# A Hymba layer on one core: residual loads, stores and sums of the out-projection on other queues and engines

## The chip, the core and the metric

The kernel runs on one core of a Trainium2 chip. The metric is device time in microseconds (us). The core has TensorE (PE), VectorE (DVE), ScalarE (ACT), GpSimd (POOL) and SyncE (SP), each with its own instruction queue that is worked off in order. SP does nothing here but issue DMAs; GpSimd issues some DMAs beside its arithmetic.

## The reference

One layer of a Hymba decoder trunk, batch 1, 1024 tokens of width 1024 behind 16 meta tokens, all in fp32.

```python
h = concat([meta, x], axis=1)
u = rmsnorm(h, attn_norm_w)
gq, gk, gv, gz, gb, ga, fq, fk, fv, ff = split(u @ w_in)
o_gdn = gated_deltanet_group(concat([gq, gk, gv]), gz, gb, ga, ...)   # 4 heads of 128, chunked delta rule
o_fox = forgetting_attention_group(fq, fk, fv, ff, fgate_b)           # 8 heads of 64, softmax with a forget bias
h = h + concat([o_gdn, o_fox], axis=-1) @ w_out
h = h + swiglu(rmsnorm(h, ffn_norm_w), w_gate, w_up, w_down)          # hidden width 2816
return rmsnorm(h, final_norm_w)[:, N_META:]
```

The change touches the lines around `h + concat(...) @ w_out`. The two halves of that product, over `o_gdn` and over `o_fox`, are computed at different times.

## The kernel before

An fp32 product is made of three matmuls: each operand is split into a high and a low part (`split`, L165 on ScalarE and L166 on VectorE), and high x high, high x low and low x high are summed in PSUM. The stages, by their place in the profiled span: the first norm and in-projection, the gated-DeltaNet group up to about 430 us, attention from 435 to 580, the out-projection from there to about 658, and the feed-forward part to the end.

Tokens go in eight tiles of 128 (`tt`). Output columns go in two halves of 512 (`nb`). The order of TensorE's instructions is written out by hand, from a list of chains and fillers with estimated times (`od`). The other engines' order is set by a scheduler that simulates a timeline; `tc.issue_after(ins)` is a hint to it that what follows is issued after `ins`.

*During attention.* `scores` computes a block of scores into a PSUM tile `sc` (two of them in turn), VectorE reduces it into `pr` with a minimum `sm` (L1060), and ScalarE takes the exponential. Between these, TensorE is filled with the GDN half of the out-projection, `wout_gdn(nb, tt)`: a residual tile `ht` (five buffers) is loaded from `x` on GpSimd's queue (L1220), twelve matmuls make `wog`, VectorE adds it to `ht` (L1223), and GpSimd stores the sum to the array `h_d` in HBM (L1224). The eight tiles of `nb=0` and one of `nb=1` run there, and another after attention. The loads of the next head (`att_head`: `kk`, `sa`, `ka`, `qa`, `avt`, `vm`) are issued on SP.

*After attention.* For the tiles in the order 0, 4, 1, 5, 2, 6, 3, 7:

- `prep_load` loads attention's output `of` from `o_d` on SP (L1260); GpSimd adds its two halves (L1261). The last four of these sums are put off and run by `run_late`.
- `prep_pe` transposes the softmax's scales (`rbt`), VectorE multiplies them in (L1276), and the result is split into `ohl`.
- `load_h` loads the residual row `hst` on SP from `h_d` (L1287), or one half from `x` (L1284) and one from `h_d` (L1285).
- `out_fox(tt, nb)` makes the fox half of the product in a PSUM tile `wof` or `wx` (L204 to L206), VectorE adds it to `hst` (L1308); after the second half, `norm2` takes the sum of squares on ScalarE (L1183), a multiply-add `st_f` on VectorE (L219), a power on GpSimd (L220), and the normalized row `xn` on VectorE (L1185). The finished `hst` is stored to `h_d` on SP (L1312).
- `u_blocks(tt)` transposes `xn` (`u2t`, L1382) and splits the blocks that the feed-forward part reads (L1387, L1388 and the lines behind them).

`hst` has two buffers: tiles 0, 1, 2, 3 use one in turn, tiles 4, 5, 6, 7 the other. So a tile's load waits until the row of the tile before it in that buffer is stored. `wof` has two PSUM buffers.

In the rows of the orders below, a number behind a name tells its buffers apart: `ht_0_0` is the residual tile of `tt=0, nb=0`, `sc_0_0_1_0` a score tile of head 0, `st2_f4` the statistics of tile 4 in `norm2` (`st_f` in the trace), and `xn2_4` its normalized row (`xn`).

Of the kernel before, what the change touches and what calls it, by code (L numbers as in the profile page):

```python
# [21 lines left out]
NT = S // P  # L22
# [5 lines left out]
EPS = 1e-6  # L28
# [12 lines left out]
ORDER = (0, 4, 1, 5, 2, 6, 3, 7)  # L41
# [56 lines left out]
def tile_hymba_layer(ctx, tc, x, meta, attn_norm_w, w_in, conv_w, a_log, dt_bias, gdn_norm_w,  # L98
                     fgate_b, w_out, ffn_norm_w, w_gate, w_up, w_down, final_norm_w, out):
    nc = tc.nc  # L100
    x, out, w_in, conv_w = x[0], out[0], w_in[0], conv_w[0]
# [22 lines left out]
    def ps_v(name):  # L124
        return bank("pv", 2, name)
# [75 lines left out]
    def mm3(dst, pairs, first=True, last=True):  # L201
        n = len(pairs)
        for i, (lh, ll, rh, rl) in enumerate(pairs):
            nc.tensor.matmul(dst, lh, rh, start=(first and i == 0), stop=False)  # L204
            nc.tensor.matmul(dst, lh, rl, start=False, stop=False)
            nc.tensor.matmul(dst, ll, rh, start=False, stop=(last and i == n - 1))  # L206
# [3 lines left out]
    def mm3g(dst, pairs, us):  # L210
        n = len(pairs)
        for i, (lh, ll, rh, rl) in enumerate(pairs):
            for a, b, first, last in ((lh, rh, i == 0, False), (lh, rl, False, False), (ll, rh, False, i == n - 1)):
                nc.tensor.matmul(dst, a, b, start=first, stop=last)  # L214
                od.pe(us)
                yield

    def inv_rms(dst, ssq, n, scale, tmp):
        nc.vector.tensor_scalar(tmp, ssq, scale, EPS, op0=ALU.mult, op1=ALU.add)  # L219
        return nc.gpsimd.tensor_tensor(dst, tmp, mhalf[:tmp.shape[0], :n], op=ALU.pow)  # L220

    def bcast(ap, shape):
# [53 lines left out]
    def proj_tm(t, w, c0, n, name, tag=ps_mm):  # L276
        col, rows = tok_cols(t)
        acc = tag(name)
        mm3(acc[:rows, :n], [(uh[:, k, col:col + rows], ul[:, k, col:col + rows],
                              w[0][k][:, c0:c0 + n], w[1][k][:, c0:c0 + n]) for k in range(KT)])  # L280
        return acc
# [30 lines left out]
    for t in range(NT):  # L312
# [3 lines left out]
        acc = proj_tm(t, w, 0, 264, f"z1_{t}")  # L316
# [8 lines left out]
    acc = proj_tm(-1, w, 256, 8, "zg")  # L325
# [202 lines left out]
    V = nc.vector  # L528
# [199 lines left out]
    last, vst, fps = [None], [None], [fp]  # L728
# [103 lines left out]
    ra_ld = {}  # L832
# [344 lines left out]
    h_d = dram.tile([NT, P, D], F32, name="h_d")  # L1177

    xn_i = [None]

    def norm2(src, wb, dst, pool, nm):
        sst = pool.tile([P, 4], F32, tag="st2", bufs=2, name=f"st2_{nm}")
        nc.scalar.activation(dst, src, AF.Square, accum_out=sst[:, 0:1])  # L1183
        pw = inv_rms(sst[:, 2:3], sst[:, 0:1], 1, 1.0 / D, sst[:, 1:2])
        xn_i[0] = V.scalar_tensor_tensor(dst, src, sst[:, 2:3], wb, op0=ALU.mult, op1=ALU.mult)  # L1185
        return pw
# [1 line left out]
    def wout_w(k0, nb):  # L1188
        return w_out[P * k0:P * k0 + 256, 512 * nb:512 * nb + 512].rearrange("(k p) n -> p k n", p=P)

    wo0c = ExitStack()
    wo = wo0c.enter_context(tc.tile_pool(name="wo0", bufs=1))
    wvs = {}

    def wout_block(k0, nb, tiles=None, col=None):
        ws = ([], [])
        for i in range(2):
            hl = load_w([(wout_w(k0 + 2 * i, nb), 1024)], f"wo{k0}_{nb}{i}", tiles and tiles(i), col)
            for o, t in zip(ws, hl):
                o.extend(t[:, 512 * k:512 * k + 512] for k in range(2))  # L1200
        return ws

    def gdn_pairs(tt, nb):
        a, b, (wh, wl) = og_of("h", tt), og_of("l", tt), wvs[nb]
        return [(a[:, k], b[:, k], wh[k], wl[k]) for k in range(4)]

    h_st = []

    def wout_gdn(nb, tt):
        if nb not in wvs:  # L1210
            parts_n[0] = 2 if nb else 1
            with tc.issue_after(ra_ld[2].ins) if not nb else nullcontext():
                wvs[nb] = wout_block(0, nb, col=gnw)
            parts_n[0] = 1
            od.on("act", 2.2)
            od.on("dve", 3.2)
        cols, nbc = slice(P * tt, P * tt + P), slice(512 * nb, 512 * nb + 512)
        ht = wo.tile([P, 512], F32, tag="ht", bufs=5, name=f"ht_{tt}_{nb}")
        with tc.issue_after((h_st[-2] if len(h_st) >= 2 else last[0]).ins):
            nc.gpsimd.dma_start(ht, x[cols, nbc])  # L1220
        acc = ps_mm(f"wog_{tt}_{nb}")
        yield from mm3g(acc, gdn_pairs(tt, nb), 0.2135)
        V.tensor_add(ht, acc, ht)  # L1223
        h_st.append(nc.gpsimd.dma_start(h_d[tt, :, nbc], ht))  # L1224
        yield od.on("dve", 0.6)
# [3 lines left out]
    def wout_gdn_all(part):  # L1229
        for nb, tt in part:  # L1230
            yield from wout_gdn(nb, tt)
# [8 lines left out]
    G = nc.gpsimd  # L1240
# [2 lines left out]
    H = 512  # L1243
    RING = ("ohl_0", "ohl_1", "nwb", "hst_1", "xn2_1", "br", "ub")
    RAWS = {"g": ("hst_0", "of_0"), "u": ("xn2_0", "of_1")}
    turn, ofs, ofl, pre_u = {}, {}, {}, {}

    def wo_tile(tag, shape, bufs, nm, dt=F32, slot=None):
        turn[tag] = turn.get(tag, -1) + 1
        return wo2.tile(shape, dt, tag=slot or f"{tag}_{turn[tag] % bufs}", name=f"{tag}_{nm}")  # L1250

    late = []

    def run_late():
        while late:
            late.pop(0)()

    def prep_load(tt):
        of = wo_tile("of", [P, 8, P], 2, tt)
        ofl[tt] = nc.sync.dma_start(of, o_d[tt])  # L1260
        late.append(lambda: G.tensor_tensor(of[:, 0:4], of[:, 0:4], of[:, 4:8], op=ALU.add))  # L1261
        if len(ofs) < 4:
            run_late()
        sp_ = spread[:, len(ofs) % 2]
        nc.scalar.copy(sp_.rearrange("p m (i c) -> p (m i) c", i=2),
                       rinv[:, :, tt:tt + 1].broadcast_to([P, FH, DH]))
        ofs[tt] = of, sp_
# [11 lines left out]
        return tail[0]  # L1279

    def load_h(tt):
        ht = wo_tile("hst", [P, D], 2, tt)
        if tt in fused:
            nc.sync.dma_start(ht[:, H:], x[P * tt:P * tt + P, H:])  # L1284
            nc.sync.dma_start(ht[:, :H], h_d[tt, :, :H])  # L1285
        else:
            nc.sync.dma_start(ht, h_d[tt])  # L1287
        pre_u[tt] += (ht,)

    accs, last_h, pows2 = {}, [None], [None]  # L1290

    def fox_g(tt):
        if tt in fused:
            accs[tt] = bank("mm", 1, f"wx_{tt}")
            mm3(accs[tt], gdn_pairs(tt, 1), last=False)

    def pf_tile(i, nm, dt=F32R):
        return pfp.tile([P, D], dt, tag=f"pf{i}", name=nm)
# [1 line left out]
    xns = {}  # L1300

    def out_fox(tt, nb):
        oh, ol, ht = pre_u[tt]
        wv = wfs[nb]
        acc = accs[tt] if nb and tt in accs else ps_v(f"wof_{tt}_{nb}")
        mm3(acc, [(oh[:, k], ol[:, k], wv[0][k], wv[1][k]) for k in range(4)], first=not (nb and tt in accs))
        hb = ht[:, H * nb:H * nb + H]
        last_h[0] = V.tensor_add(hb, acc, hb)  # L1308
        if nb:
            xn = wo_tile("xn2", [P, D], 2, tt)  # L1310
            pows2[0] = norm2(ht, nwb2, xn, wo2, f"f{tt}")
            nc.sync.dma_start(h_d[tt], ht)  # L1312
            xns[tt] = xn

    for tag in RING + ("hst_0", "of_0", "xn2_0", "of_1", "s4"):
# [2 lines left out]

    nwb2 = wo2.tile([P, D], F32, tag="nwb", name="nwb2")
    spread = wo2.tile([P, 2, 4, P], F32, tag="s4", name="spread")  # L1320
    prep_load(ORDER[0])
    with tc.issue_after(last_o[0].ins):
        prep_load(ORDER[1])
# [6 lines left out]
    for _ in wout_gdn(1, 1):  # L1330
        pass
    first_o = prep_pe(ORDER[0])
    with tc.issue_after(first_o[0].ins), tc.issue_after(first_o[1].ins):
        wfs.append(wout_block(4, 1, lambda i: [pf_tile(2 * i + c, f"wf{c}_{i}") for c in range(2)]))
    with tc.issue_after(ofl[ORDER[1]].ins):
        load_h(ORDER[0])
    fox_g(ORDER[1])
    prep_load(ORDER[2])
    out_fox(ORDER[0], 0)
    prep_pe(ORDER[1])  # L1340
    with tc.issue_after(ofl[ORDER[1]].ins):
        load_h(ORDER[1])
# [224 lines left out]
    with tc.manual_schedule(engines={mybir.EngineType.PE}):  # L1567
        for i, tt in enumerate(ORDER):
# [150 lines left out]
        for n, p in enumerate(PH2):  # L1719
# [25 lines left out]
            late = [tc.issue_after(x.ins) for x in tail[0]] if p == "p4" else [nullcontext()] * 2  # L1745
# [31 lines left out]
```

## Time and profile before

| | |
|---|---|
| median of 3 runs | 1295.05 us (1294.88 to 1295.83) |
| profiled execution | 1295.79 us, its span 1294.1 us |
| mean granted TensorE clock | 0.997 of full speed |
| TensorE busy | 1276.2 us, 99% of the span |
| VectorE busy | 838.1 us, 65% |
| ScalarE busy | 548.1 us, 42% |
| GpSimd busy | 367.2 us, 28% |

A row of the timeline has the start in the span and the duration in us, the engine, the line of the kernel, the operation, what it writes and reads, and in brackets how long the engine had been idle and what released it. The table of stretches gives the busy time of each engine in a stretch, and the granted clock. Issuing a DMA counts as no busy time; "SPq" and "POOLq" are the queues in which DMAs are issued.

### The profile page before, as it was taken

To read this page: it belongs to the slowest core of one execution; us is meant where nothing else is said; L and a number is where in the kernel's file an instruction comes from. 1 tells how busy PE (TensorE), PEld (TensorE's weight loads), DVE (VectorE), ACT (ScalarE), POOL (GpSimd) and SP (SyncE) were. 2 spreads that over 40 slices of the span, in tenths; PEclk is the share of its full clock that TensorE was granted. 3 is DMA by queue.
4 is the path that set the end of the run, shared out by engine and by line. 5 is a ranking of instruction groups with operands and counts; after the bars stand their busy time and mean duration, and the time that the engine had idled before them with its cause. 6 is when DMAs were issued, how large, how long until landed. Compare 5 with 4: busy or idle time off the path is not lost.

```text
span 1294.1 us, 19940 instructions
## 1 busy us (share of the span) xinstructions
PE 1276.2 (99%) x7418; PEld 1125.9 (87%) x7418; DVE 838.1 (65%) x1511; ACT 548.1 (42%) x943; POOL 367.2 (28%) x343
## 2 busy tenths in 40 slices
PE   9999999999999999999999999999999999999998
PEld 8999999999999888887778888888888888888887
DVE  6567899465266588876887666655656654465645
ACT  6455434142234477874453323333333343433333
POOL 2012213102323222213405534455433443020301
PEclk9999999999999999999999999999999999999999
DMA  6433634666499678837434554554445467955513
GB/s 231 133 112 118 178 93 105 187 191 216 165 327 273 195 208 228 226 80 261 163 131 154 194 164 147 178 187 131 146 156 168 156 212 268 395 183 201 206 63 130
DMA packets 181840, 234.90 MB, mean 182 GB/s; under 512 B 19160, under 2 KB 132080, under 8 KB 178928
## 3 DMA queue, kind: packets, MB, share of 16 engines
q1 hardware_dynamic: 176048, 215.74, 52.1%
q0 software_dynamic: 5696, 17.90, 4.2%
q8 instruction: 58, 0.95, 0.3%
q14 instruction: 38, 0.31, 0.1%
HBM read 154.68 MB, written 78.92 MB: 181 GB/s over the span
## 4 chain that ended last, share of the span: by engine, by line
PE 87%; DVE 5%; DMA 3%; issue 2%; ACT 2%; SPq 1%; POOL 0%; POOLq 0%; DVEq 0%; ACTq 0%
PE xp L1658 9%; PE yp L1658 7%; PE ua L1483 5%; PE ga L1483 5%; PE gb L1483 5%; PE ud L1483 5%; PE gd L1483 5%; PE ub L1483 5%; PE pj_fq L214 4%; PE pj_fk L214 3%; PE pt L1101 2%; PE ue L1483 2%; PE ge L1483 2%; PE fv L214 2%; PE wog L214 2%
## 5 line engine op out<-in xcount | busy, mean ns | idle before, releaser
L166 DVE TENSOR_TENSOR al_p<-ra_p,ah_p 128x2048 fp32r<-128x2048 f32 (+1 forms) x21 | 47.2, 2250 | 95.1 <-ACT ah_p L165 95.1
L165 ACT CAST ah_p<-ra_p 128x2048 fp32r<-128x2048 f32 (+1 forms) x21 | 37.1, 1767 | 106.3 <-PE xp L1658 46.5
L1658 PE MATMUL xp<-wl_p,ah_p 128*128 128x512 f32 (+1 forms) x176 | 67.3, 382 | 0.0
L1658 PE MATMUL xp<-wh_p,al_p 128*128 128x512 f32 (+1 forms) x176 | 67.3, 382 | 0.0
L1658 PE MATMUL xp<-wh_p,ah_p 128*128 128x512 f32 (+1 forms) x176 | 67.3, 382 | 0.0
L1539 POOL TENSOR_TENSOR gzw<-gzw,uzt 128x512 f32<-128x512 f32 x11 | 18.1, 1649 | 169.7 <-DVE uzt L1528 113.0
L1483 PE MATMUL gb<-uh_p,w_g_p 128*128 128x512 f32 x176 | 57.8, 389 | 0.0
L1483 PE MATMUL ub<-uh_p,w_u_p 128*128 128x512 f32 x176 | 57.8, 389 | 0.0
L1483 PE MATMUL gd<-uh_p,w_g_p 128*128 128x512 f32 x176 | 57.8, 389 | 0.0
L1483 PE MATMUL ud<-uh_p,w_u_p 128*128 128x512 f32 x176 | 57.8, 389 | 0.0
L1539 POOL TENSOR_TENSOR gxy<-gxy,uxy 128x512 f32<-128x512 f32 x22 | 38.9, 1767 | 64.5 <-DVE uxy L1528 42.4
L165 ACT CAST ph<-pt 128x512 fp32r<-128x512 f32 (+1 forms) x96 | 45.4, 478 | 24.9 <-PE pt L1101 22.3
L166 DVE TENSOR_TENSOR pl<-pt,ph 128x512 fp32r<-128x512 f32 (+1 forms) x96 | 52.0, 553 | 4.5 <-ACT ph L165 4.0
L1065 ACT ACTIVATE pr<-pr,sm 128x144 f32<-128x144 f32 (+3 forms) x64 | 50.6, 793 | 9.6 <-DVE sm L1060 9.3
L166 DVE TENSOR_TENSOR w_u_p<-raw_u,w_u_p 128x512 fp32r<-128x512 f32 x42 | 41.0, 977 | 20.3 <-ACT w_u_p L165 20.1
L1483 PE MATMUL ga<-uh_p,w_g_p 128*128 128x512 f32 x160 | 52.5, 389 | 0.0
L1483 PE MATMUL ua<-uh_p,w_u_p 128*128 128x512 f32 x160 | 52.5, 389 | 0.0
L1658 PE MATMUL yp<-wh_p,ah_p 128*128 128x512 f32 x132 | 51.3, 389 | 0.0
L1658 PE MATMUL yp<-wl_p,ah_p 128*128 128x512 f32 x132 | 51.3, 389 | 0.0
L1658 PE MATMUL yp<-wh_p,al_p 128*128 128x512 f32 x132 | 51.3, 389 | 0.0
L165 ACT CAST w_u_p<-raw_u 128x512 fp32r<-128x512 f32 x42 | 26.0, 620 | 55.3 <-PE gd L1483 35.6
L166 DVE TENSOR_TENSOR wl_p<-rw_p,wh_p 128x2048 fp32r<-128x2048 f32 (+1 forms) x21 | 46.5, 2213 | 3.9 <-ACT wh_p L165 3.9
(654 smaller groups left out, 4246.2 us busy)
## 6 DMA issues: line engine op xcount, KB each, us to landing
ra_p<-ao_p SPq DMA_DIRECT2D x14, 1024.0 KB
raw_g<-in_w_gate_dram SPq DMA_DIRECT2D x22, 512.0 KB
raw_u<-in_w_up_dram SPq DMA_DIRECT2D x22, 512.0 KB
raw_d<-in_w_down_dram SPq DMA_DIRECT2D x22, 512.0 KB
wt_p<-raw_d SPq DMA_DIRECT2D x33, 256.0 KB
rw_p<-wt_p SPq DMA_DIRECT2D x8, 1024.0 KB
rw_p<-in_w_down_dram SPq DMA_DIRECT2D x6, 1024.0 KB
ao_p<-gzw SPq DMA_DIRECT2D x22, 256.0 KB
```

The lines of the kernel that those rows point to most:

```text
L165: cast = nc.scalar.copy(dst_hi, src)
L166: low = nc.vector.tensor_sub(dst_lo, src, dst_hi.bitcast(F32))
L214: nc.tensor.matmul(dst, a, b, start=first, stop=last)
L1065: nc.scalar.activation(pr[:, :n], pr[:, :n], AF.Exp, bias=sm[:, np_ - 1:np_], scale=-1.0, accum_out=rsum[:, h, j:j + 1])
L1101: nc.tensor.transpose(pt[:, P * j:P * j + P], pts[j][0][:, j, c0:c0 + P], ident)
L1483: nc.tensor.matmul(dst, a[:, c], b[:, k], start=(first and k == 0 and i == 0), stop=(k == 3 and i == 2), skip_group_check=not first)
L1539: last_mul[0] = G.tensor_tensor(gs[d], gs[d], us[d], op=ALU.mult)
L1658: nc.tensor.matmul(dst[:, n_], a[:, f, c], b[:, f, n_], start=(first and i == 0 and n == 0), stop=(i == NF - 1 and n == 2), skip_group_che ...
```

## The change

It has five parts, all around the residual and attention's output; TensorE's instructions and their order stay as they are.

1. The `ht` tiles of the first two blocks (`tt` 0 and 1, `nb` 0) are made before the second head's loads and loaded on SP ahead of them; before, they were loaded on GpSimd at the start of attention.
2. `load_h` of the first tile stands ahead of the `of` loads, without the hint that kept it behind the second of them.
3. The `h_d` stores of the first two tiles in the order (0 and 4) are issued on GpSimd instead of SP.
4. The sums of the halves of `of` for the last four tiles (2, 6, 3, 7) are made on VectorE, behind the `xn` that was made last, instead of on GpSimd.
5. The first add of the last tile (7) is issued behind the `st_f` multiply-add of tile 3.

```diff
+    ms_i = [None]
+
     def inv_rms(dst, ssq, n, scale, tmp):
-        nc.vector.tensor_scalar(tmp, ssq, scale, EPS, op0=ALU.mult, op1=ALU.add)
+        ms_i[0] = nc.vector.tensor_scalar(tmp, ssq, scale, EPS, op0=ALU.mult, op1=ALU.add)
         return nc.gpsimd.tensor_tensor(dst, tmp, mhalf[:tmp.shape[0], :n], op=ALU.pow)
...
+    wo0c = ExitStack()
+    wo = wo0c.enter_context(tc.tile_pool(name="wo0", bufs=1))
+
+    def ht_tile(tt, nb):
+        return wo.tile([P, 512], F32, tag="ht", bufs=5, name=f"ht_{tt}_{nb}")
+
+    ht01 = [ht_tile(tt, 0) for tt in range(2)]
+    with tc.issue_after(ra_ld[NT - 1].ins):
+        for tt in range(2):
+            nc.sync.dma_start(ht01[tt], x[P * tt:P * tt + P, 0:512])
     with tc.issue_after(last[0].ins):
         att_tiles(1)
     hds[1] = att_head(1)
...
-        ht = wo.tile([P, 512], F32, tag="ht", bufs=5, name=f"ht_{tt}_{nb}")
-        with tc.issue_after((h_st[-2] if len(h_st) >= 2 else last[0]).ins):
-            nc.gpsimd.dma_start(ht, x[cols, nbc])
+        if ht01:
+            ht = ht01.pop(0)
+        else:
+            ht = ht_tile(tt, nb)
+            with tc.issue_after(h_st[-2].ins):
+                nc.gpsimd.dma_start(ht, x[cols, nbc])
...
-        late.append(lambda: G.tensor_tensor(of[:, 0:4], of[:, 0:4], of[:, 4:8], op=ALU.add))
+
+        def halves_sum():
+            with tc.issue_after(xn_i[0].ins) if len(ofs) > 3 else nullcontext():
+                (V if len(ofs) > 3 else G).tensor_tensor(of[:, 0:4], of[:, 0:4], of[:, 4:8], op=ALU.add)
+
         if len(ofs) < 4:
-            run_late()
+            halves_sum()
+        else:
+            late.append(halves_sum)
...
-        last_h[0] = V.tensor_add(hb, acc, hb)
+        with tc.issue_after(ms_i[0].ins) if tt == ORDER[-1] and not nb else nullcontext():
+            last_h[0] = V.tensor_add(hb, acc, hb)
         if nb:
             xn = wo_tile("xn2", [P, D], 2, tt)
             pows2[0] = norm2(ht, nwb2, xn, wo2, f"f{tt}")
-            nc.sync.dma_start(h_d[tt], ht)
+            (nc.gpsimd if nst[0] < 2 else nc.sync).dma_start(h_d[tt], ht)
+            nst[0] += 1
...
+    load_h(ORDER[0])
     prep_load(ORDER[0])
...
-    with tc.issue_after(ofl[ORDER[1]].ins):
-        load_h(ORDER[0])
     fox_g(ORDER[1])
```

The scheduler's answer to it is seen in the order of instructions. VectorE at the start of attention, before:

```order
L1060 ISA sm_1_0_4_5067 128x1
L1223 TENSOR_TENSOR ht_0_0_5004<-wog_0_0_5006,ht_0_0_5004 128x512
L1060 ISA pr_1_0_5066,sm_1_0_4_5067<-sc_1_0_4_1_5075,zmask_5022,sm_1_0_4_5067 128x328
L1060 ISA sm_1_0_4_5067 128x1
L1060 ISA pr_1_0_5066,sm_1_0_5_5080<-sc_1_0_5_0_5081,zmask_5022 128x392
L1060 ISA sm_1_0_5_5080 128x1
L1223 TENSOR_TENSOR ht_1_0_5040<-wog_1_0_5042,ht_1_0_5040 128x512
```

And in the changed kernel, where `ht_0_0` is now:

```order
L800 SCALAR_TENSOR_TENSOR fhl_fq3_700_4981<-pj_fq3_700_4956,fhl_fq3_700_4981 128x340
L1236 TENSOR_TENSOR ht_0_0_4865<-wog_0_0_5008,ht_0_0_4865 128x512
L1072 ISA pr_0_0_5023,sm_0_0_0_5029<-sc_0_0_0_0_5030,zmask_5024 128x144
L1072 ISA sm_0_0_0_5029 128x1
L1072 ISA pr_0_0_5023,sm_0_0_1_5035<-sc_0_0_1_0_5036,zmask_5024 128x272
```

The first add has moved from behind the fifth score block to a place ahead of the first score reduction; the second add (`ht_1_0`) stays where it was.

GpSimd in the out-projection, at tiles 0 and 4, before:

```order
L1261 TENSOR_TENSOR of_4_7102<-of_4_7102 128x512
L1261 TENSOR_TENSOR of_1_7175<-of_1_7175 128x512
L220 TENSOR_TENSOR st2_f0_7220<-st2_f0_7220,mhalf_94 128x1
L1261 TENSOR_TENSOR of_5_7226<-of_5_7226 128x512
L220 TENSOR_TENSOR st2_f4_7323<-st2_f4_7323,mhalf_94 128x1
```

And in the changed kernel:

```order
L1277 TENSOR_TENSOR of_4_7104<-of_4_7104 128x512
L1277 TENSOR_TENSOR of_1_7175<-of_1_7175 128x512
L1331 DMA h_d_4995<-hst_0_7098 128x1024
L222 TENSOR_TENSOR st2_f0_7220<-st2_f0_7220,mhalf_94 128x1
L1277 TENSOR_TENSOR of_5_7226<-of_5_7226 128x512
L1331 DMA h_d_4995<-hst_4_7202 128x1024
L222 TENSOR_TENSOR st2_f4_7323<-st2_f4_7323,mhalf_94 128x1
```

Each of the two stores now stands between a sum of `of` and the power of `norm2`.

VectorE a little later, at tiles 1 and 5, before:

```order
L1185 SCALAR_TENSOR_TENSOR xn2_4_7322<-hst_4_7202,st2_f4_7323,nwb2_7096 128x1024
L1276 TENSOR_TENSOR of_5_7226<-rbt_5_7361,of_5_7226 128x512
L166 TENSOR_TENSOR ohl_5_7360<-of_5_7226,ohl_5_7360 128x512
L1308 TENSOR_TENSOR hst_1_7307<-wof_1_0_7346,hst_1_7307 128x512
L1308 TENSOR_TENSOR hst_1_7307<-wof_1_1_7375,hst_1_7307 128x512
```

And in the changed kernel:

```order
L1197 SCALAR_TENSOR_TENSOR xn2_4_7322<-hst_4_7202,st2_f4_7323,nwb2_7096 128x1024
L1327 TENSOR_TENSOR hst_1_7307<-wof_1_0_7346,hst_1_7307 128x512
L1295 TENSOR_TENSOR of_5_7226<-rbt_5_7361,of_5_7226 128x512
L166 TENSOR_TENSOR ohl_5_7360<-of_5_7226,ohl_5_7360 128x512
L1327 TENSOR_TENSOR hst_1_7307<-wof_1_1_7375,hst_1_7307 128x512
```

The first add of tile 1's residual row now stands ahead of the multiply of tile 5. On SP's queue its load (`hst_1`) stands ahead of the `of` load of tile 2 and of the residual loads of tile 5, since the two stores that stood there have left.

More of the change, by code (lines that the diff above doesn't have):

```diff
@@ L1189, in wout_w @@
         return w_out[P * k0:P * k0 + 256, 512 * nb:512 * nb + 512].rearrange("(k p) n -> p k n", p=P)
-    wo0c = ExitStack()
-    wo = wo0c.enter_context(tc.tile_pool(name="wo0", bufs=1))
     wvs = {}
@@ L1245, in tile_hymba_layer @@
     RAWS = {"g": ("hst_0", "of_0"), "u": ("xn2_0", "of_1")}
-    turn, ofs, ofl, pre_u = {}, {}, {}, {}
+    turn, ofs, ofl, pre_u, h_in = {}, {}, {}, {}, {}
     def wo_tile(tag, shape, bufs, nm, dt=F32, slot=None):
@@ L1281, in load_h @@
     def load_h(tt):
-        ht = wo_tile("hst", [P, D], 2, tt)
+        ht = h_in[tt] = wo_tile("hst", [P, D], 2, tt)
         if tt in fused:
@@ L1287, in load_h @@
             nc.sync.dma_start(ht, h_d[tt])
-        pre_u[tt] += (ht,)
-    accs, last_h, pows2 = {}, [None], [None]
+    accs, last_h, pows2, nst = {}, [None], [None], [0]
     def fox_g(tt):
@@ L1302, in out_fox @@
     def out_fox(tt, nb):
-        oh, ol, ht = pre_u[tt]
+        (oh, ol), ht = pre_u[tt], h_in[tt]
         wv = wfs[nb]
```

## The prediction

> **What bounds the kernel now.** I read the page first, its line of busy times.
>
> ```profile
> PE 1276.2 (99%) x7418; PEld 1125.9 (87%) x7418; DVE 838.1 (65%) x1511; ACT 548.1 (42%) x943; POOL 367.2 (28%) x343
> ```
>
> TensorE (PE) is busy for 1276.2 of 1294.1 us, and the change adds, drops and reorders none of its instructions. So only the time in which TensorE waits, or runs below its full clock, can be won. The second view is the table of stretches. Each row gives the stretch, its length, the busy time of PE, of its weight loads, of DVE, ACT and POOL, then the granted clock, the DMA share and GB/s.
>
> ```profile
> 440.00:448.00 8.00, 5.48 (x21) 3.93 (x20) 5.15 (x15) 3.75 (x8) 2.18 (x4) 0.79 0.44 157
> 600.00:608.00 8.00, 6.84 (x37) 5.53 (x35) 4.92 (x8) 3.95 (x8) 1.86 (x2) 1.00 0.83 256
> 616.00:625.00 9.00, 8.67 (x42) 6.64 (x41) 7.13 (x9) 5.53 (x10) 3.40 (x3) 1.00 0.39 139
> 644.00:658.00 14.00, 13.15 (x66) 10.80 (x66) 11.06 (x18) 9.14 (x17) 0.55 (x1) 1.00 0.38 119
> ```
>
> These are the stretches that the change touches. TensorE stands still for 2.52 us at attention's start (440 to 448), where the granted clock is also low, and for 1.16, 0.33 and 0.85 us in the out-projection. The third view is the same table in four neighbouring pieces of 3.4 us; three of them:
>
> ```profile
> 440.50:443.90 3.40, 1.17 (x4) 0.60 (x4) 2.56 (x7) 0.93 (x2) 1.09 (x2) 1.00 0.20 77
> 443.90:447.30 3.40, 3.11 (x10) 2.66 (x11) 1.89 (x7) 2.13 (x4) 1.10 (x2) 0.50 0.72 247
> 447.30:450.70 3.40, 3.40 (x23) 2.91 (x21) 2.88 (x11) 1.89 (x5) 0.00 (x0) 1.00 0.05 16
> ```
>
> A piece in which TensorE is busy for only 1.17 of 3.40 us is followed by one at a granted clock of 0.50. That costs a second time: 3.11 us of busy time at half clock hold what takes about 1.55 us at full clock. Fourth, the timelines of TensorE, GpSimd (POOL) and VectorE (DVE) around it, which say who is waited for (in brackets: idle time before, and what ended it).
>
> ```profile
> 442.56 0.44 PE L1055 MATMUL sc<-ka,qa 70*128 70x392 f32 x1 [2.06 <-DVE sm L1060]
> 444.19 0.75 PE L1055 MATMUL sc<-ka,qa 70*128 70x456 f32 x1 [0.46 <-DVE sm L1060]
> ...
> 435.54 0.74 POOL L800 DMA_DIRECT2D q_d<-fhl_fq  x1 [1.37 <-DVE fhl_fq L798]
> 436.27 1.14 POOL L1220 DMA_DIRECT2D ht<-in_x_dram  x2
> ...
> 441.34 0.69 DVE L1223 TENSOR_TENSOR ht<-wog,ht 128x512 f32<-128x512 f32 x1 [2.25 <-DMA ht<-in_x_dram]
> 442.90 0.69 DVE L1223 TENSOR_TENSOR ht<-wog,ht 128x512 f32<-128x512 f32 x1
> ```
>
> The residual tile `ht` is asked for at 436.27, behind q_d's store on GpSimd's queue, and VectorE's in-order queue stands 2.25 us for it. The score reductions behind that add keep their two PSUM buffers, so the next score matmul waits 2.06 us, and a later one 0.46.
>
> **The change part by part.**
>
> *Two residual tiles on SP.* They are issued ahead of kk_1, where SP's queue now stands at 418 us, 17 us before the first add can run. The two issues cost SP about 1.2 us. The cover is SP's own pause:
>
> ```profile
> 424.50 4.82 SPq L755 DMA_DIRECT2D vm<-vz_d  x4
> 449.19 0.24 SPq L765 DMA_DIRECT2D ka<-c_d  x1
> ```
>
> SP ends at 429.3 and issues nothing until 449.2, so what slips is absorbed there, and I cost the issues at nothing. If the loads of the second head were needed before 430, each us of slip would be a us of wait. GpSimd loses 1.14 us of issuing, in time that nobody waits for.
>
> What is late next? The adds themselves stay in VectorE's queue. The first now stands ahead of the first score reduction, the second where it was.
>
> ```profile
> 434.97 0.39 PE L214 MATMUL wog<-whi_wo,ul_p 128*128 128x512 f32 x1
> 436.14 0.38 PE L1055 MATMUL sc<-ka,qa 70*128 70x400 f32 x1
> 440.10 0.40 PE L214 MATMUL wog<-whi_wo,ul_p 128*128 128x512 f32 x1
> ...
> 435.70 0.31 DVE L1060 CUSTOM_DVE_ANT_0 pr<-sc,zmask 128x144 f32<-128x144 f32 x1 [0.57 <-PE sc L1056]
> 443.51 0.62 DVE L1060 CUSTOM_DVE_ANT_0 pr<-sc,zmask,sm 128x392 f32<-128x392 f32 x1
> ```
>
> The first add can start when its last matmul ends, 434.97 + 0.39 = 435.36, and takes 0.69, so the first reduction (0.31, and 0.08 to read its sum) ends at about 436.5 instead of 436.0; the third score matmul, now at 436.14, waits about 0.3. The second add can start at 440.5 (440.10 + 0.40) and holds back the reduction of 0.62 behind it to about 442.0, while TensorE would want its buffer at about 441.4: about 0.6. The first delay eats part of the second, so I put both at 0.8 (0.6 to 1.0). Gain at attention's start: 2.06 + 0.46 + 1.55 - 0.8 = 3.3 us, with 2.4 and 4.1 as ends.
>
> *The out-projection's load and stores.* TensorE's four waits there, and the chain that ended last:
>
> ```profile
> 592.74 0.47 PE L204 MATMUL wof<-whi_wo,ohl 128*128 128x512 f32 x1 [0.40 <-DVE hst L1308]
> 607.94 0.47 PE L204 MATMUL wof<-whi_wo,ohl 128*128 128x512 f32 x1 [1.16 <-DVE hst L1308]
> 624.34 1.07 PE L1382 MATMUL u2t<-ident,xn 128*128 128x128 f32 x8 [0.33 <-DVE xn L1185]
> 654.18 1.06 PE L1382 MATMUL u2t<-ident,xn 128*128 128x128 f32 x8 [0.85 <-DVE xn L1185]
> ...
> 582.01 2.72 DMA o_d<-oa
> 585.66 6.22 DMA hst<-h_d
> 595.02 6.86 DMA h_d<-hst
> 601.94 5.07 DMA hst<-h_d
> ```
>
> The first row `hst_0` of the residual is issued at 585.66 behind the `of` and `nwb` loads. Ahead of them it waits for nothing of attention's last head's output, so it lands many us before its add: the 0.40 goes wholly. Tile 1 uses tile 0's buffer, so its load at 601.94 waits for the store issued at 595.02, which took 6.86 us on SP. On GpSimd the store stands behind of_1's sum and ahead of the `pow`:
>
> ```profile
> 595.20 1.28 POOL L1261 TENSOR_TENSOR of<-of 128x512 f32<-128x512 f32 x1 [4.82 <-DVE st_f L219]
> ...
> 603.47 0.68 DVE L1276 TENSOR_TENSOR of<-rbt,of 128x512 f32<-128x512 f32 x1
> 604.23 0.62 ACT L165 CAST ohl<-of 128x512 fp32r<-128x512 f32 x1 [0.38 <-DVE of L1276]
> ...
> o_d<-oa POOLq DMA_DIRECT2D x32, 128.0 KB, 5.5
> q_d<-fhl_fq POOLq DMA_DIRECT2D x8, 342.0 KB, 7.6
> h_d<-ht POOLq DMA_DIRECT2D x10, 256.0 KB, 4.3
> ```
>
> The store is ready no earlier than 593.4 and no later than this sum's end, 596.5, less the 0.40: 596.1. I take 594.7, since of_1's load loses 512 KB that stood ahead of it. No row has a 512 KB store on this queue. Bounds from above: 2.72 (the o_d row) and 7.6 us (q_d); I take 5.0, between the 4.3 of the nearest row, the same destination at half the size, and the 5.5 of o_d. The store then lands at 599.7, and the load of hst_1, 5.07 us at most with less ahead of it in its queue (I take 4.2), at 603.9.
>
> What waits for it has changed too: hst_1's first add now stands ahead of of_5's multiply. So wof_5 needs landing + 0.69 (add) + 0.68 (multiply) + 0.62 (cast), with gaps 2.1 us. TensorE is free for it at 607.94 - 1.16 - 0.40 = 606.4, so a landing up to 604.3 costs nothing. The early end (593.4 + 2.72 + 4.2 = 600.3) frees all 1.16; the late end (596.1 + 7.6 + 5.07 = 608.8) makes the wait 4.5. Central: 1.16 less about 0.3 for a margin this thin. The stores' issue delays the `pow` of tiles 0 and 4 by about 0.6; their next use lies over 2 us behind, so I cost it at nothing, and at 0.2 if not.
>
> *Sums of the last four tiles on VectorE, and the late add.*
>
> ```profile
> L1185 DVE SCALAR_TENSOR_TENSOR xn<-hst,st_f,nwb x8: 1274/1698/2317, 597.3 to 661.7; 128x1024 f32<-128x1024 f32 x8
> ...
> 621.83 1.29 POOL L1261 TENSOR_TENSOR of<-of 128x512 f32<-128x512 f32 x1
> 621.89 2.30 DVE L1185 SCALAR_TENSOR_TENSOR xn<-hst,st_f,nwb 128x1024 f32<-128x1024 f32 x1
> ```
>
> The xn multiply takes 1.27 us alone and up to 2.32 beside GpSimd's sum. Each of four sums adds a 0.69 instruction to VectorE behind xn and takes away 1.0 of xn: the xn is earlier by 1.0, which frees the 0.33 at 624.34, and what is behind it by 0.3. Moving the last tile's add (0.69) behind the multiply-add of tile 3 brings that tile's chain, and so the 0.85 at 654.18, forward by about 0.7. Some new waits of 0.1 or 0.2 from the reordering (ohl behind the wx add) I take as 0.3 in all. Out-projection: 0.40 + 0.86 + 0.33 + 0.70 - 0.3 = 2.0 us, with 2.8 (nothing late) and -1.8 (late end of the store) as ends.
>
> **Sum.** 3.3 + 2.0 = 5.3 us. The profiled execution took 1295.79 us, 1.7 more than its span of 1294.1, and 0.74 more than the median of 1295.05. So 1290.5 against the profiled one, and 1289.8 against the median; I give 1289.9.
>
> **Rivals.**
>
> (1) *The GpSimd store lands late.* If it takes what the same transfer took on SP, 6.86, hst_1 lands at 594.7 + 6.86 + 5.07 = 606.6 and the wait is 2.3 instead of 1.16. The out-projection then gains nothing (2.0 - 2.0), and the time is 1291.8. For it: 342 KB on that queue took 7.6. Against it: the SP store stood behind two weight loads and an `of` load of its own queue. The Trainium skill, page "SBUF — State Buffer", section "SBUF: two separate sides", speaks for it: descriptors of a GpSimd-issued DMA are written by GpSimd and starve while VectorE runs an operation that takes the shared port, and it advises the SP queue. No row here separates that from traffic.
>
> (2) *The clock still dips.* If the half clock at 443.9 isn't due to the wait, the 1.55 stays: 1291.5. Against it: the stretch 600 to 608, with 1.16 us idle, kept 1.00, and the dip follows the emptiest piece. The Trainium skill, page "TensorE: Matmul & The Clock Gate", section "What's actually happening", has the clock fall after a whole idle window of about 3.4 us. By that rule a 2.06 us gap could not have caused this dip, and closing it need not remove it; the trace, with 1.17 us busy ahead of the dip, differs.
>
> (3) *Attention's start stays bound by VectorE.* If the adds delay scores as much as the load did, only the out-projection's 2.0 is left: 1293.1. Against it: VectorE was busy only 2.56 of 3.40 us even there.
>
> (4) *Slower: the store holds SP's queue.* hst_1's load now stands ahead of of_2, hst_5 and of_6. To cancel the other 5.0 us (5.3 without its 0.3) the wait needs about 3.5 us, since a gap of that size would bring its own half-clock piece (1.55). That is a landing of hst_1 at 607.8, of the store at 603.6 at my load time: 8.9 us after issue, beyond the longest row, 7.6. At 12 us after issue the wait is 6.6 and the time 1297.6, slower by 0.2%.
>
> **How the numbers follow.** Forecast 0.61, rival 1 0.21, rival 2 0.08, rival 3 0.06, rival 4 0.04. About 0.2% of the time, 2.6 us, is what a measurement of this kernel can tell from no change, so faster means below 1292.5. The forecast's own range is 1288.0 (all waits gone, 4.1 + 2.8 = 6.9, less a little) to 1291.2; with rivals 1 and 2 it reaches 1292.4. Faster: 0.61 + 0.19 + 0.08 = 0.88, less 0.01 of the forecast; same: 0.06 and the rest of rival 1, with 0.01, 0.09; slower 0.04.
>
> **What the profile of the changed kernel would show.** Right: no 0.50 piece near 444; the waits of `sc` for `sm` under 0.7 each; the two `ht` adds with no wait for a DMA; no `wof` wait of 0.40 at tile 0; the GpSimd store landing about 5 us after its issue and the hst_1 add without a DMA wait; `xn` at about 1.28 us in all eight. Wrong: an `of` multiply of tile 5 or `ohl` late behind hst_1; a half-clock piece elsewhere; a wait of the second head for kk_1. The weakest step is the store's landing: two us later, and the out-projection's gain is gone.

## The result and the profile after

The changed kernel runs in 1292.45 us (median of 14 runs, 1291.29 to 1296.61), the kernel before in 1294.84 (14 runs beside them). The ratio is 0.9983, with a 95% interval of 0.9975 to 0.9991: about 2.4 us faster, where 5.2 were forecast, and just outside the forecast's range (1288.0 to 1292.4). The profiled execution took 1292.73 us, its span is 1291.0. The two profiles are 3.1 us apart and not 2.4, since that of before was one of the longer executions of its kernel. Two of the runs of the experiments below, of 2565 and 3266 us at full clock, are in none of the ratios.

The table of stretches of the changed kernel (busy PE, PEld, DVE, ACT, POOL, then granted clock, DMA share, GB/s):

```profile
440.00:448.00 8.00, 7.45 (x46) 6.22 (x45) 6.82 (x22) 5.88 (x14) 1.08 (x2) 1.00 0.26 83
592.00:600.00 8.00, 7.09 (x38) 5.54 (x37) 7.20 (x9) 4.42 (x8) 3.41 (x5) 1.00 0.76 249
600.00:608.00 8.00, 7.84 (x42) 6.09 (x41) 4.70 (x9) 3.61 (x7) 0.89 (x2) 1.00 0.75 232
608.00:616.00 8.00, 6.37 (x33) 4.99 (x31) 8.00 (x9) 4.11 (x9) 4.86 (x3) 1.00 0.42 152
616.00:625.00 9.00, 8.63 (x43) 6.86 (x44) 6.58 (x11) 5.58 (x10) 0.55 (x1) 1.00 0.56 171
644.00:658.00 14.00, 14.00 (x66) 11.45 (x65) 12.28 (x21) 9.60 (x18) 0.84 (x2) 1.00 0.48 163
```

The start of attention is as forecast: 0.55 us idle in 440 to 448 where 2.52 were, and a full clock. The out-projection is not. Its four old waits are gone, but 0.91 us is lost in 592 to 600 and 1.63 in 608 to 616, where VectorE (the third busy time) works for 8.00 of 8.00 us. TensorE's timeline gives the new waits:

```profile
442.57 0.47 PE L1067 MATMUL sc<-ka,qa 70*128 70x456 f32 x1 [0.55 <-DVE sm L1072]
597.34 0.50 PE L206 MATMUL wof<-whi_wo,ohl 128*128 128x512 f32 x1 [0.91 <-DVE ohl L166]
604.19 0.50 PE L204 MATMUL wof<-whi_wo,ohl 128*128 128x512 f32 x1 [0.16 <-ACT ohl L165]
615.96 0.50 PE L204 MATMUL wof<-whi_wo,ohl 128*128 128x512 f32 x1 [1.63 <-ACT ohl L165]
617.06 0.50 PE L206 MATMUL wof<-whi_wo,ohl 128*128 128x512 f32 x1 [0.37 <-DVE ohl L166]
```

All of them wait for `ohl`, the split of attention's output: of tile 1 (597), tile 5 (604) and tile 2 (616 and 617). They add up to 3.07 us; the old ones were 0.40 + 1.16 + 0.33 + 0.85, and 0.09 in smaller ones. The out-projection has traded its waits.

With TensorE's timeline cut at the first `sc`, the first `rbt` and the first `ga`, the span falls into four parts (us):

| profiled execution | to attention | attention | out-projection | feed-forward |
|---|---|---|---|---|
| before | 435.20 | 147.64 | 75.01 | 636.23 |
| changed | 435.64 | 144.04 | 75.13 | 636.22 |

The change takes 3.60 us out of attention and nothing out of the out-projection. (The 0.44 us to attention lies far ahead of anything changed: in this execution a piece of 3.41 us at half clock stood at 12 us of the span, in that of before it didn't.)

VectorE ahead of the wait of 1.63 us, and GpSimd beside it, in the changed kernel:

```profile
602.15 0.69 DVE L1327 TENSOR_TENSOR hst<-wof,hst 128x512 f32<-128x512 f32 x1 [2.22 <-DMA hst<-h_d]
607.89 2.12 DVE L1197 SCALAR_TENSOR_TENSOR xn<-hst,st_f,nwb 128x1024 f32<-128x1024 f32 x1
609.93 1.77 DVE L1277 TENSOR_TENSOR of<-of 128x512 f32<-128x512 f32 x1
614.53 0.68 DVE L1295 TENSOR_TENSOR of<-rbt,of 128x512 f32<-128x512 f32 x1
...
607.63 1.29 POOL L1429 TENSOR_TENSOR br<-br,ub 128x512 f32<-128x512 f32 x1
608.89 3.98 POOL L1407 TENSOR_TENSOR ul_p<-br,uh_p 128x512 fp32r<-128x512 f32 x2
```

`xn` of tile 1 still takes 2.12 us: GpSimd's sum has left, but its `br` block has moved up into the sum's place, 0.26 us ahead of `xn`. The sum itself, now on VectorE, takes 1.77 us beside GpSimd's `ul_p`, not 0.69. Behind both stand the add and three `ul_p`, and only then, at 614.53, the multiply that `ohl` of tile 2 needs.

### The profile page after: what moved, and what is told of

Same layout as the page of the kernel before. It is cut to its first block, busy times and chain, and to the rows that moved or that the text cites. A ratio compares the mean times of both kernels' runs of the same rounds, so it can differ in the third digit from the quotient of the medians.

```text
span 1291.0 us, 19941 instructions
## 1 busy us (share of the span) xinstructions
PE 1275.0 (99%) x7418; PEld 1126.0 (87%) x7418; DVE 840.0 (65%) x1515; ACT 548.4 (42%) x943; POOL 362.4 (28%) x339
## 4 chain that ended last, share of the span: by engine, by line
PE 88%; DVE 4%; DMA 3%; issue 2%; SPq 1%; ACT 1%; POOL 0%; POOLq 0%; DVEq 0%; ACTq 0%
PE xp L1677 9%; PE yp L1677 7%; PE ua L1502 5%; PE ga L1502 5%; PE gb L1502 5%; PE ud L1502 5%; PE gd L1502 5%; PE ub L1502 5%; PE pj_fq L214 4%; PE pj_fk L214 3%; PE pt L1113 2%; PE ue L1502 2%; PE ge L1502 2%; PE wog L214 2%; PE fv L214 2%
```

## The experiments

**The kernel before, again,** to see what its executions differ in.

> The kernel before, unchanged, to see what its executions differ in. Theory A (the half-clock piece behind the 2.06 us wait belongs to some executions only, as it depends on where the wait falls in the clock's windows): the times spread over about 1.6 us, with granted clocks of 0.997 and of 0.998 or more side by side, and a second profile may show no 0.50 piece near 444 although the 2.06 us wait is there. Theory B (the wait brings it every time): every profile has it, and the times cluster within 1 us.

Median 1295.35 us of 11 runs, against 1294.79 beside them (ratio 1.0002, 0.9993 to 1.0011). Its profile has the wait of 1.89 us and a longer piece at half clock behind it, as the granted clock in the stretch shows:

```profile
440.00:448.00 8.00, 6.14 (x19) 4.68 (x20) 5.56 (x16) 3.87 (x8) 2.18 (x4) 0.64 0.43 138
```

In the profile of before, the half clock held for 3.41 us from 443.9; here for 6.83 us from 442.3, and attention took 148.63 instead of 147.64. All runs of the kernel before beside the experiments, 82 with these, have granted clocks of 0.996 to 0.999, with median times of 1296.1 (12 runs at 0.996), 1295.5 (34 at 0.997), 1294.5 (28 at 0.998) and 1293.1 us (8 at 0.999). So executions differ in their pieces of half clock, as Theory A has it, and from the fastest group to the median of all, 1295.0, it is 2.0 us. But the piece behind this wait stood in each profile that has the wait, as Theory B has it; that the fastest runs have none was not seen.

The out-projection takes 74.31 us in this profile and 75.01 in the first, with waits of 0.15 and 0.83 for `hst` in place of 0.40 and 1.16. So stage times of single profiles, here and below, differ by 0.7 us without any edit.

**Part 1 alone.** The kernel before, with the two `ht` tiles on SP.

```diff
+    ht01 = [ht_tile(tt, 0) for tt in range(2)]
+    with tc.issue_after(ra_ld[NT - 1].ins):
+        for tt in range(2):
+            nc.sync.dma_start(ht01[tt], x[P * tt:P * tt + P, 0:512])
```

> The kernel before with part 1 alone (two ht tiles on SP). Theory A (the attention stage is where the whole gain comes from): 2.4 to 3.5 us faster than before, as much as the whole change; TensorE's idle in 440 to 448 falls from 2.5 to about 0.6 us, and the out-projection's waits stay at 0.40, 1.16, 0.33 and 0.85. Rival (the parts help each other, and part 1 alone is worth only the 2.06 us wait): under 2 us.

1291.73 us against 1294.79, ratio 0.9979 (0.9970 to 0.9988): 3.1 us, at least as much as the whole change, though the two intervals overlap. Attention takes 144.15 us; the out-projection keeps three of its old waits (0.68, 0.32, 0.84) and takes 74.02. Its ten runs lie within 1.7 us of each other, the 82 of before within 4.9.

**Parts 2 to 5 alone.** The changed kernel with `ht` loaded on GpSimd as before.

> The changed kernel without part 1, so parts 2 to 5 alone. Theory A (the out-projection trades its waits for new ones): within 0.5 us of before, TensorE idle in the out-projection 2.8 to 3.2 us, with waits for ohl of about 0.9, 1.6 and 0.4 in place of those for hst and xn. Rival (what the prediction said): 2.0 us faster.

1295.30 us against 1294.79, ratio 1.0004 (0.9994 to 1.0014): nothing gained. TensorE waits 0.93, 1.61 and 0.37 us for `ohl`, at the same three places as in the changed kernel. In this profile the wait for tile 2 brought a half-clock piece of its own:

```profile
616.00:625.00 9.00, 7.02 (x24) 4.96 (x23) 5.73 (x10) 4.34 (x8) 1.38 (x2) 0.81 0.42 133
```

**Tile 2's sum back on GpSimd,** the three others left on VectorE.

```diff
-                (V if len(ofs) > 3 else G).tensor_tensor(...)
+                (V if on_v else G).tensor_tensor(...)    # on_v: the last three tiles
```

> The changed kernel with the sum of tile 2 alone back on GpSimd (tiles 6, 3 and 7 stay on VectorE). Theory A (that sum, in the stretch where VectorE was busy 8.00 of 8.00 us, is what makes ohl of tile 2 late): the waits of 1.63 and 0.37 us before wof of tile 2 shrink to under 0.5 together, and the time is 1.2 to 2 us below the changed kernel's, about 3.5 to 4.5 us below before. Rival (VectorE is late there for the load of hst_1 and for GpSimd's blocks beside it, whoever makes the sum): waits within 0.5 us of the changed kernel's, no gain.

1290.40 us, ratio 0.9967 (0.9956 to 0.9979). Of the 2.0 us before `wof` of tile 2 a single 0.46 is left, and the multiply stands at 611.05 instead of 614.53 (the stage itself begins 0.6 us earlier here):

```profile
606.45 1.30 POOL L1279 TENSOR_TENSOR of<-of 128x512 f32<-128x512 f32 x1
...
606.71 2.12 DVE L1197 SCALAR_TENSOR_TENSOR xn<-hst,st_f,nwb 128x1024 f32<-128x1024 f32 x1
611.05 0.67 DVE L1297 TENSOR_TENSOR of<-rbt,of 128x512 f32<-128x512 f32 x1
...
614.08 0.50 PE L206 MATMUL wof<-whi_wo,ohl 128*128 128x512 f32 x1 [0.46 <-DVE ohl L166]
```

The sum on GpSimd takes 1.30 us, and `xn` of tile 1 is 2.12 us with it or without it: VectorE is spared the 1.77 and loses nothing. The out-projection falls from 75.13 to 72.75 us. Of these 2.4, 0.6 are there before tile 2: the add that waits for hst_1 starts 21.89 us after the first `rbt` here and 22.47 in the changed kernel's execution. The other 1.8 are at tile 2, and they are the sum together with the order that came with it: two `ul_p` stand ahead of the multiply here, as before the change, and three in the changed kernel (0.60 us). That is the lost gain; the medians of the runs are 2.05 us apart. Some of it is given back later: the feed-forward part takes 637.61 instead of 636.2, with a wait of 1.12 us near 725.

**All four sums back on GpSimd** (part 4 undone).

> The changed kernel with all four moved sums back on GpSimd (part 4 undone). With tile 2's sum alone back there the time was 1290.4. Theory A (only tile 2's sum hurts on VectorE, the other three help): the multiply xn is slow again (2.3 us) for tiles 5, 2, 6, waits of u2t for xn of 0.3 and 0.2 to 0.9 us come back, time 1290.9 to 1291.6. Rival (the other three sums are worth nothing either): 1290.4 within 0.3.

1291.50 us, ratio 0.9976 (0.9968 to 0.9985); the out-projection takes 73.45, 0.7 more than with three sums on VectorE. `u2t` waits again for `xn`, 0.32 and 0.24 us, and `xn` has 1.69 us as its median and 2.31 as its longest. So the three other moved sums seem to be worth something together. It is not clear of the noise: 0.7 us is what two profiles of one kernel differed by, and the two intervals overlap.

**Stores back on SP** (part 3 undone), with tile 2's sum on GpSimd.

```diff
-            (nc.gpsimd if nst[0] < 2 else nc.sync).dma_start(h_d[tt], ht)
+            nc.sync.dma_start(h_d[tt], ht)
```

> The changed kernel with tile 2's sum on GpSimd and the two h_d stores back on SP (part 3 undone). Theory A (the store on GpSimd is what brings hst_1 earlier): hst_1's add waits for its DMA again and wof of tile 5 waits about 1.2 us or more, since its multiply now stands behind that add; time 1291.4 to 1292.4. Rival (a late load is covered, the store's queue does not matter): 1290.4 within 0.3.

1290.02 us, ratio 0.9967 (0.9956 to 0.9979), out-projection 72.53: no worse. The rival was right: hst_1's add waits for its DMA, as it also does with the stores on GpSimd, and TensorE waits 0.34 us for `ohl` of tile 5, not 1.2. SP's queue here, and GpSimd's and SP's in the kernel with the stores on GpSimd:

```profile
589.71 0.42 SPq L1333 DMA_DIRECT2D h_d<-hst  x1
596.02 0.32 SPq L1308 DMA_DIRECT2D hst<-h_d  x1
...
591.22 0.57 POOL L1333 DMA_DIRECT2D h_d<-hst  x1
596.50 0.34 SPq L1308 DMA_DIRECT2D hst<-h_d  x1
```

From the store's issue to the load that waits for it 6.3 us pass on SP and 5.3 on GpSimd. But GpSimd issues it 1.5 us later (1.1 counted from the first `rbt`), as its queue first waits for the `of` load of tile 1 and makes that sum. Either way hst_1 is asked for at about 596, and the add that waits for it starts 21.7 or 21.9 us after the first `rbt`.

**The first residual load back behind the `of` loads** (part 2 undone), with tile 2's sum on GpSimd.

> The changed kernel with tile 2's sum on GpSimd and the first residual load back behind the of loads (part 2 undone). VectorE's order goes back to that of before at tiles 0 and 1: the multiply of tile 1 ahead of xn of tile 0. Theory A (the early load removes 0.40 but its new order of VectorE costs 0.9 at ohl of tile 1): the 0.9 us wait is gone, the 0.40 is back, time 1289.6 to 1290.2. Rival (the early load is a gain of 0.4): 1290.8 or more, and the wait for ohl of tile 1 stays.

1290.54 us, ratio 0.9969 (0.9957 to 0.9981), out-projection 72.94. Of the 0.40 us wait 0.23 comes back, and the 0.9 for `ohl` of tile 1 is gone: VectorE's order is that of before again. Counted from the first `rbt`, TensorE is 0.48 us behind the kernel with the early load after tile 0, 0.56 ahead of it after tile 1, and 0.07 behind again at tile 5. So the early load did what it should, and the order that it brought cost more, but what is won at tile 1 without that order is given back at tile 5. The stage is no shorter than with the early load (72.75), and the time is the same, where 1289.6 to 1290.2 was expected.

**xn of tile 0 behind the multiply of tile 1,** the early load kept.

```diff
+        mul = V.tensor_mul(of[:, 0:4], pt, of[:, 0:4])
+        while put_off:                      # xn of the first tile
+            with tc.issue_after(mul.ins):
+                put_off.pop()()
```

> The changed kernel with tile 2's sum on GpSimd, and xn of tile 0 issued behind the multiply of tile 1, everything else kept, the early load too. Theory A: the wait of 0.91 us for ohl of tile 1 falls under 0.2, time 1289.3 to 1289.8, the fastest so far. Rival (the wait comes from GpSimd's sum of tile 5, which runs beside ohl's low part and makes it 1.6 us, not from the order): the wait stays at 0.5 or more, time 1290.4 within 0.3.

The wait of 0.89 us is gone and the out-projection falls to 72.29, but the time is 1290.72 us (0.9970, 0.9958 to 0.9982), as without this edit. TensorE is 1.08 us ahead after tile 1, and gives back more than half of that at tile 5. The feed-forward part takes 637.69, with the wait near 725 at 1.19 us:

```profile
724.52 0.47 PE L1514 MATMUL gd<-uh_p,w_g_p 128*128 128x512 f32 x1 [1.19 <-DVE gzw L1559]
...
718.27 0.69 DVE L1496 TENSOR_TENSOR ws_u<-raw_u,raw_u 128x512 f32<-128x512 f32 x1 [2.97 <-DMA raw_u<-in_w_up_dram]
```

VectorE waits there 2.97 us for a weight load. That wait stands in some of the faster kernels' profiles (0.5 to 1.2 us) and not in others; what decides it was not tried.

**Part 3 alone undone,** tile 2's sum still on VectorE.

> The changed kernel with only part 3 undone: the two stores back on SP, tile 2's sum still on VectorE. Theory A (the waits in the out-projection are in a row on one VectorE chain that starts when hst_1 lands, so removing the first lengthens the later one): the 0.9 us wait for ohl of tile 1 goes, the wait for ohl of tile 2 grows to 2.5 us or more, the stage from the first rbt to the first ga stays within 0.4 of the changed kernel's 75.1 us, time 1292.1 to 1292.8. Rival (the waits are separate and add up): the stage falls to 74.2 and the time to 1291.5.

1292.24 us, ratio 0.9980 (0.9971 to 0.9988), as the changed kernel. The out-projection takes 75.54, but with a half-clock piece of 3.41 us at 615.5 in it, and the 0.9 us wait did not go, it is 0.96. So the run can't tell whether the waits add up; the two runs above say that they don't in full. It tells what the 0.9 is. Here are VectorE's split of tile 1 and GpSimd's sum of tile 5, in this kernel and then in the one with the stores on SP and tile 2's sum on GpSimd, whose order on VectorE is the same at this place:

```profile
594.72 1.60 DVE L166 TENSOR_TENSOR ohl<-of,ohl 128x512 fp32r<-128x512 f32 x1
594.48 1.29 POOL L1277 TENSOR_TENSOR of<-of 128x512 f32<-128x512 f32 x1 [3.00 <-DMA of<-o_d]
...
594.70 0.68 DVE L166 TENSOR_TENSOR ohl<-of,ohl 128x512 fp32r<-128x512 f32 x1
594.80 1.73 POOL L1279 TENSOR_TENSOR of<-of 128x512 f32<-128x512 f32 x1 [3.15 <-DMA of<-o_d]
```

Where GpSimd's sum started first, by 0.24 us, the split took 1.60 us and the sum 1.29. Where the split started first, by 0.10 us, it took 0.68 and the sum 1.73, and TensorE did not wait at all. The Trainium skill, page "SBUF — State Buffer", section "SBUF: two separate sides", has VectorE and GpSimd take a shared port pair as a lock: a VectorE operation with two SBUF inputs and a GpSimd operation that reads SBUF block each other, whoever starts first has it for the whole instruction. These four rows agree. In all seven profiles in which this sum started first, by 0.22 to 0.73 us, the split ended 1.82 to 1.84 us after the sum's start: it waits for the end of the sum, 1.28 to 1.29 us long, and then needs some 0.55. So the wait of 0.9 is this collision. The new order makes it possible, since it puts the split at the moment when the `of` load of tile 5 lands; with the old order the two don't meet.

**The multiply of tile 5 first,** on the kernel with stores on SP and tile 2's sum on GpSimd: tile 1's first add issued behind `ohl` of tile 5, as it stood before the change.

```diff
+                if put_add:                 # the first add of tile 1
+                    with tc.issue_after(sp5[1].ins):
+                        put_add.pop()()
```

> The fastest so far (stores on SP, tile 2's sum on GpSimd) with the first add of tile 1 put behind ohl of tile 5 on VectorE, as it stood before the change. Theory A (the add that waits for hst_1's load blocks the multiply of tile 5): the wait of 0.34 us before wof of tile 5 goes, the stage falls from 72.5 to 72.2 us, time 1289.4 to 1290.0. Rival (wof then waits for the PSUM buffer that the later add frees): a wait of 0.3 or more for hst at the same place, no change.

1290.13 us, ratio 0.9967 (0.9955 to 0.9980). The wait of 0.34 is gone, as Theory A has it, but in this profile GpSimd's sum was first again, and 0.91 for `ohl` of tile 1 stands in its place. The stage takes 72.33.

**The two `ht` adds later** in VectorE's order, on top of that.

```diff
+        if not nb and tt < 2:
+            held.append(finish)             # add and store, issued in the middle of the next block
```

> As the kernel with the multiply of tile 5 first, and the first two ht adds put later in VectorE's order: the first behind the sixth score reduction, the second behind the first head's reductions. Theory A (what is left of the wait at attention's start is the two adds of 0.69 us in VectorE's queue): the waits of sc for sm near 437 and 442 (0.22 and 0.55 us) go, the stage from the first sc to the first rbt falls from 144.1 to 143.3 to 143.6 us, time 0.5 to 0.8 below its sibling. Rival (VectorE is the bound there with its reductions, wherever the adds stand): 144.1 within 0.2.

1288.62 us, ratio 0.9957 (0.9945 to 0.9970). Attention takes 143.12 us, 1.0 less, a little more than expected: the waits of 0.55 at attention's start and of 0.58 near 481 and 518 are gone, one of 0.19 stays.

**All of these together,** with xn of tile 0 behind the multiply of tile 1 too.

> The fastest kernel so far with xn of tile 0 put behind the multiply of tile 1, so that ohl's low part of tile 1 is ahead of the hst add and about 1.5 us earlier, before GpSimd's sum of tile 5 starts. Theory A (the 0.9 us wait is VectorE's split, 0.68 us alone, running beside GpSimd's sum, and comes or goes with 0.1 us of the of load's landing): the split takes 0.7 us, the wait of 0.96 is gone, the stage from the first rbt to the first ga falls from 72.3 to 71.4 to 71.7; time 1287.7 to 1288.4 unless the feed-forward part waits 0.5 to 1.2 us for gzw. Rival (GpSimd's sum only meets another VectorE operation, and as much is lost there): the stage stays at 72.3 within 0.2.

1287.92 us against 1295.17, ratio 0.9945 (0.9931 to 0.9959): the fastest here. The split meets no sum any more, and TensorE is 1.2 us ahead of the kernel above after tile 1. Yet the stage takes 72.65, since TensorE now waits at tile 2:

```profile
593.07 0.68 DVE L166 TENSOR_TENSOR ohl<-of,ohl 128x512 fp32r<-128x512 f32 x1
594.32 1.29 POOL L1298 TENSOR_TENSOR of<-of 128x512 f32<-128x512 f32 x1 [2.98 <-DMA of<-o_d]
...
607.94 0.69 DVE L1356 TENSOR_TENSOR hst<-wof,hst 128x512 f32<-128x512 f32 x1 [1.83 <-DMA hst<-h_d]
...
612.24 0.50 PE L204 MATMUL wof<-whi_wo,ohl 128*128 128x512 f32 x1 [1.01 <-ACT ohl L165]
613.35 0.50 PE L206 MATMUL wof<-whi_wo,ohl 128*128 128x512 f32 x1 [0.37 <-DVE ohl L166]
```

The rival was right about the stage, but not about the cause: the sum took its 1.29 us and met nothing. VectorE stands 1.83 us for the load of tile 5's residual row, ahead of the multiply of tile 2; in the kernel above it doesn't wait there. SP issues that load at 602.60 here and at 601.11 there. It waits for the store of tile 4, which the scheduler has put behind the `of` load of tile 2 (596.15, the store at 596.57) and not ahead of it (the store at 595.91). So an edit on VectorE's order was paid for by the order that it gave SP's queue; that was not tried by itself. The times of these two kernels, 0.7 us apart, are not told apart by the two intervals.

## Why the prediction was wrong, and where it was right

*Right: attention's start.* It forecast 3.3 us, with 0.8 us of waits left over from the adds. The stage gave 3.60 in the profiles, part 1 alone 3.1 in the runs, and the wait left over was 0.55. The half-clock piece was in the sum with 1.55; TensorE's idle time from 440 to 448 fell by 1.97, which leaves 1.63 for it. Behind this wait the piece stands in both profiles of before and in that of parts 2 to 5 alone, and in no profile of a kernel that has part 1. Rival 2 and rival 3 fall.

*Right for the store, short for the load behind it, and lucky in the wait.* The store was to be issued at 594.7 in the old time, to land 5.0 us later, and hst_1's load to take 4.2, at most 5.07. In the changed kernel, whose first `rbt` is 3.16 us earlier, the store is issued at 591.86, the load that waits for it follows at 596.96, and the add at 602.15:

```profile
591.86 0.57 POOL L1331 DMA_DIRECT2D h_d<-hst  x1
596.96 0.34 SPq L1306 DMA_DIRECT2D hst<-h_d  x1
```

That makes 5.1 and 5.2. In the old time hst_1 lands at 605.3, 1.0 past the 604.3 that was to cost nothing. That TensorE waits only 0.16 us for it, at 604.19, is luck: its new wait at tile 1 had made TensorE itself 0.8 us later than forecast (free at 607.2 in the old time instead of 606.4). So neither rival 1 nor rival 4 is what happened. But the 0.86 us was not the store's to give: with it on SP, the kernel is as fast.

*Wrong, and the step that failed: the sums of the last four tiles.* It read: "Each of four sums adds a 0.69 instruction to VectorE behind xn and takes away 1.0 of xn". For the sums of tiles 6 and 7 that is what happened: 0.68 us each, behind an `xn` of 1.28 and 1.27 instead of 2.30. For tile 2 the sum added 1.77 and took away nothing (`xn` of tile 1: 2.12, before 2.11), and TensorE waited 2.0 us. For tile 3 it added 1.77 too and took away 0.65 (`xn` of tile 2: 1.67, before 2.32); there no wait followed. The row that the step rested on, `xn` at 2.30 beside GpSimd's sum at 621.83, belongs to a tile behind whose sum GpSimd has nothing else to do. Behind the sums of tiles 2 and 3 it has blocks of `br` and `ul_p`, as the timeline of before shows; the sums on VectorE in the changed kernel stand below it:

```profile
611.81 2.29 POOL L1410 TENSOR_TENSOR br<-br,ub 128x512 f32<-128x512 f32 x1
621.83 1.29 POOL L1261 TENSOR_TENSOR of<-of 128x512 f32<-128x512 f32 x1
631.73 1.30 POOL L1261 TENSOR_TENSOR of<-of 128x512 f32<-128x512 f32 x1
632.98 2.27 POOL L1388 TENSOR_TENSOR ul_p<-br,uh_p 128x512 fp32r<-128x512 f32 x1
...
621.48 0.68 DVE L1277 TENSOR_TENSOR of<-of 128x512 f32<-128x512 f32 x1
629.92 1.67 DVE L1197 SCALAR_TENSOR_TENSOR xn<-hst,st_f,nwb 128x1024 f32<-128x1024 f32 x1
631.51 1.77 DVE L1277 TENSOR_TENSOR of<-of 128x512 f32<-128x512 f32 x1
640.76 0.68 DVE L1277 TENSOR_TENSOR of<-of 128x512 f32<-128x512 f32 x1
```

With the sum gone from GpSimd, these blocks start in its place, and slow the same `xn` and the sum on VectorE behind it. Putting tile 2's sum back takes 1.8 us out of the out-projection at tile 2, of the 2.1 by which that stage missed its forecast (2.0 forecast, -0.1 measured).

*Wrong in size: the new waits from the reordering,* put at 0.3 in all, were 0.91, the collision of the split with GpSimd's sum. What the other moves won came as forecast or better: no wait for `xn` is left, and TensorE, 2.02 us behind its place of before once it has waited for `ohl` of tile 2, is only 0.14 behind it at the stage's end. No run leaves out the move of the last add alone; with it, and with all four sums on GpSimd, the last wait for `xn` is 0.24 where it was 0.85. The median of `xn` fell from 1698 to 1284 ns:

```profile
L1197 DVE SCALAR_TENSOR_TENSOR xn<-hst,st_f,nwb x8: 1273/1284/2116, 593.1 to 658.7; 128x1024 f32<-128x1024 f32 x8
```

The longest, 2116 ns, is that of tile 1.

The total: in the profiles 3.6 won at attention and nothing net in the out-projection, where 3.3 and 2.0 were forecast. The rivals of the prediction all put the risk on DMAs, the clock or the first stage; none had VectorE as the bound of the out-projection, though the change put four sums on it. (In rival 4 the two figures don't fit each other: by the terms that give its 1297.6, the wait that cancels the gain is 4.05 us, not 3.5.)

## What to carry to other kernels

A price taken from one instance of a repeated step holds for the others only if their neighbours are the same: look at what both engines do around each of the instances before multiplying. When a step is moved off an engine, ask what on that engine moves up into its place, and whether that collides with the same work. A wait that is removed ahead of a busy engine can be paid again further on, as happened here at tile 5 when the wait at tile 1 went.

## What the runs showed of the hardware

Two operations that both read SBUF, one on VectorE and one on GpSimd, slowed each other by what came first: 0.68 us against 1.60 for the same split, and 1.29 against 1.73 for the same sum, decided by which of them started 0.10 or 0.24 us ahead of the other.

The half clock comes in pieces of 3.41 us, one or two of them, and not only after the 2 us wait: waits of 1.61 and 0.37 brought one in the kernel with parts 2 to 5 alone and waits of 1.22 and 0.36 in the one with part 3 undone, while 1.63 and 0.37 in the changed kernel's profile did not. Within one execution the pieces begin on one grid: at 11.92 and 1288.50 us in the changed kernel's profile, 374 times 3.413 apart; at 443.39 and 620.87 in that of parts 2 to 5 alone, 52 times; at 615.48 and 1287.91 in that with part 3 undone, 197 times. Cut by this grid, the stretch from 430 to 660 us of all 14 profiles shows after which windows a full clock falls to half: after the five in which TensorE was busy for 1.17, 1.22, 1.52, 1.59 and 1.83 us, and not after one of 1.79 or any of 2.20 or more. So a window that is about half empty was enough here, and where a wait falls in the grid matters; 1.79 and 1.83 are too near each other to give a bound. Why a second piece follows in two of the profiles is open.

The Trainium skill, page "TensorE: Matmul & The Clock Gate", section "What's actually happening", has windows of 3413 ns that run freely, which fits the length and the grid. The same section of the Trainium skill has the clock fall after an idle window; read as a window without any work, that does not fit, since TensorE was busy for 1.17 of the 3.40 us ahead of the piece in the profile of before.
